# Down projection of a hybrid layer: finished blocks turned to frames by VectorE in 32x32 blocks that the stores put in place, instead of by TensorE

## Chip, cores and metric

One core of a Trainium2 chip. The time is the device time of one execution in microseconds (us). Engines: TensorE (PE, its weight loads PEld), VectorE (DVE), ScalarE (ACT), GpSimd (POOL), SyncE (SP). Times inside an execution come from the profile of one execution and count from the start of its span.

## The reference, cut to what matters

One streaming step of a layer for 512 prompt frames and 64 sample frames (576 together, 2048 channels, all float32): a projection into attention and convolution groups, an output projection, and a SwiGLU feed-forward. The change touches the last line alone:

```python
x = x + mix @ w_out
h2 = rmsnorm(x, g_norm2)
x = x + (jax.nn.silu(h2 @ w_gate) * (h2 @ w_up)) @ w_down     # w_down: 5632 x 2048
```

The result goes to two tensors, `y_prompt` (512 x 2048) and `y_sample` (64 x 2048), frame by row.

## The kernel before, in words

Everything is kept with channels on the 128 partitions and frames along the row, so the down phase ends with blocks of 128 channels x 288 frames that must be turned before they are stored as rows of frames.

**Work units.** The down phase computes 8 column groups `d` of 256 channels. Each gives four blocks `(c, i)`: `c` is which 128 of its channels, `i` which half of the frames (`HALVES`: 0 to 287 and 288 to 575). The hidden pairs arrive over time, so `DOWN` (L44) is a hand-written list of 37 visits `(d, first pair, last pair)`; a visit works on m pairs. The last eight visits, 29 to 36 here, finish the groups d = 0, 1, 3, 6, 7, 5, 2, 4 with m = 5, 5, 5, 5, 5, 6, 4, 4, and only they store. A group's multiplication is done by a seven-product (Strassen-Winograd) scheme: products 1 to 7, each of 3m matmuls (`multiply`, L400; three matmuls a pair, from a high and a low part of each operand). The order (L1517 to L1522) is, around visit n: (n+1, 1), (n, 3), (n, 4), (n+1, 2), (n+1, 6), (n+1, 7), (n+1, 5), and for the last visit (36, 4), (36, 3).

**What ends a block** (`run`, L421 to L477). Block (0,0) is done after product 2, (1,1) after product 5, (0,1) after product 3, (1,0) after product 4. DVE adds the PSUM result to the block (`add`, L449), POOL adds the copies `part` that ACT keeps (L451). Products 7 and 4 share one PSUM tile `psw`: 4 is accumulated upon 7, so TensorE may start product 4 only when DVE has read product 7 for block (1,1) (L449).

**Weights.** A visit's weights come in one transfer of m x 256 KB into one of two regions (`load_columns`, L327, on SP), as soon as the splits of products 3 and 4 of the visit that used the region are done. `prepare` (L357) makes the high part by ACT (L227) and the low part by DVE (L228) four products ahead (`AHEAD`, L1621), into four buffers; the weight sums of the scheme are DVE's too (L344 to L352).

**Order.** From the last gate and up unit on, the program order is each engine's order (`manual_schedule`, L1627): an instruction that waits holds up all that follows on its engine. DMAs issued from SP and ACT report on eight completion counters in turn; a DMA waits until the one eight before it has landed.

**The store** (`store_y`, L1579) is a generator in `Pipeline` (L73). One tick is one pair of a product (three matmuls); a generator runs when as many ticks have gone by as it yielded. Nine ticks after its block is done, TensorE turns it in three pieces against an identity matrix (L1598) into one of two PSUM tiles; three ticks on, ACT copies 256 frames back over the block (L1601) and the last 32 into one of four small tiles `obs` (L1603); four ticks on, the stores are issued: two on SP for i = 0 (L1606, L1589), four for i = 1, whose frames go over from `y_prompt` to `y_sample` at frame 512 (L1589, L1591). The stores of the last visit are shared among SP, ACT and POOL.

Of the kernel before, what the change touches and what calls it, by code (L numbers as in the profile page):

```python
# [10 lines left out]
F32 = mybir.dt.float32  # L11
# [5 lines left out]
P = 128  # L17
TP = 512
TS = 64
T = TP + TS  # L20
HALF = T // 2
HALVES = ((0, HALF), (HALF, T))
D = 2048
KD = D // P
NH = 8
# [10 lines left out]
NFP = NFF // 2  # L36
DC = D // 256
SLOTS = 7
# [63 lines left out]
def tile_hybrid_stream_step(  # L102
# [6 lines left out]
    nc = tc.nc  # L109
# [5 lines left out]
    yp, ys = y_prompt[0], y_sample[0]  # L115
# [24 lines left out]
    def misc(name):  # L140
        return ps_z.tile([P, 512], F32, tag="misc", name=name, bufs=2)
# [3 lines left out]
    for half in (1, 0):  # L145
        for c in range(D // 256):
            specs.append((w_out[half * AW : (half + 1) * AW, c * 256 : (c + 1) * 256]
# [7 lines left out]
    NU = len(gu)  # L155
# [38 lines left out]
    def next_weight():  # L194
        i = pos[0]
        pos[0] += 1
        end = first_block
        def pieces_of(j):
            hi, lo = weight_split(j)
            for a in range(0, 2048, 512):  # L200
                weight_parts(raws[j][:, :2048], hi, lo, a, a + 512, nc.vector)
                yield 7

        while len(raws) < min(i + 2, end):
            load_weight()
        if len(ready) <= i:
            split_weight(nc.vector)
        while len(raws) < min(i + 3, end):
            load_weight()
        if i + 1 < end:  # L210
            pipe.spawn(pieces_of(i + 1))
            pipe.run_due()
        out = ready[i]
        ready[i] = None
        return out
# [20 lines left out]
    ident = const.tile([P, P], F32, name="ident")  # L236
# [4 lines left out]
    rows = {}  # L241
# [72 lines left out]
    def load_columns(gone=(), one=False):  # L314

        free.extend(gone)
        while wanted and room(*wanted[0]) and (one or not hold):
            n, c = wanted.pop(0)
            one = False
            src, wide_, m = source(n, c)  # L320
            halves = room(n, c)
            for h in halves:
                free.remove(h)
            t = raw_tile[halves[0][0]]
            t = t[:, halves[0][1], :] if len(halves) == 1 else t.rearrange("p h e -> p (h e)")
            t = t[:, : 2 * m * wide_]
            nc.sync.dma_start(out=t.rearrange("p (k e) -> p k e", e=wide_), in_=src)  # L327
            if c is None:
                v = t.rearrange("p (j s h c) -> p j s h c", s=2, h=2, c=P)
                region[n, 0], region[n, 1] = (v[:, :, :, 0, :], halves), (v[:, :, :, 1, :], ())  # L330
            else:
                region[n, c] = t.rearrange("p (j s c) -> p j s c", s=2, c=P), halves
# [216 lines left out]
    def turn_x(kt, low=None):  # L549
# [25 lines left out]
        if q == 0:  # L575
            for (a, b), d in zip(HALVES, (b11[:, j], b12a[:, j] if j < NP - 1 else b12b)):
                nc.scalar.activation(out=d[:, 0, :], in_=st[:, 0, a:b], func=AF.Copy, scale=g)
# [54 lines left out]
    with tc.manual_schedule(engines={mybir.EngineType.Activation, mybir.EngineType.DVE, mybir.EngineType.SP}):  # L632
# [60 lines left out]
        for kt in range(KD + LAG):  # L693
# [22 lines left out]
            if kt in (7, 11, 17):  # L716
                j = (kt - 7) // 4
# [7 lines left out]
        for c in range(2):  # L725
            for i, (a, b) in enumerate(HALVES):
                if i:
# [12 lines left out]
        for kt in range(KD):  # L740
# [6 lines left out]
            if kt == 9:  # L747
                nc.vector.reduce_sum(out=ssr, in_=ssx, axis=mybir.AxisListType.X)
                nc.vector.tensor_scalar(out=ssr, in0=ssr, scalar1=1.0 / D, scalar2=EPS, op0=ALU.mult, op1=ALU.add)
                nc.gpsimd.tensor_tensor(out=rst, in0=ssr, in1=nhalf, op=ALU.pow)  # L750
# [15 lines left out]
    for c in range(2):  # L766
        for i, (a, b) in enumerate(HALVES):
            nc.scalar.copy(out=e1[c][:, a:b], in_=v1ps[c][i])
# [81 lines left out]
    def group_scale(acc_, bufs):  # L850
        for a, b in HALVES:
            ss = misc("ssg")[:, :HALF]
            mm(ss, oner.bitcast(F32), acc_[:, a:b], start=True, stop=True)
            yt = tmp.tile([P, 2, HALF], F32, tag="hl", name="ytg", bufs=bufs)
            y, t = yt[:, 0], yt[:, 1]
            nc.scalar.activation(out=ss, in_=ss, func=AF.Identity, scale=1.0 / (8 * P), bias=epsc)
            nc.scalar.activation(out=y, in_=ss, func=AF.Ln)
            nc.scalar.activation(out=y, in_=y, func=AF.Exp, scale=-0.5)
            nc.scalar.activation(out=t, in_=y, func=AF.Square)
            nc.vector.scalar_tensor_tensor(out=t, in0=t, scalar=-0.5, in1=ss, op0=ALU.mult, op1=ALU.mult)  # L860
            nc.vector.scalar_tensor_tensor(out=acc_[:, a:b], in0=t, scalar=1.5, in1=y, op0=ALU.add, op1=ALU.mult)
            yield 1
# [11 lines left out]
    def a_done(n, c, i, ps, part):  # L874
        kind, g = UNITS[n][:2]
        a, b = HALVES[i]
        if kind in ("v", "qk"):
# [189 lines left out]
    for h in range(NH):  # L1067
        t = tpool.tile([P, 2, T], F32R, tag=f"t{h}", name=f"mixa{h}")
# [5 lines left out]
    def out_proj(frame, R, after=None, before=None, first=None):  # L1074
        for c in range(D // 256):
            whi, wlo = first[0] if first and c == 0 else next_weight()
            load_x2()
            if before:
                before(c)
            for j in range(2):  # L1080
                kt = 2 * c + j
                for a, b in HALVES:
                    if first and kt == a == 0:
                        ps = first[1]
                    else:
                        ps = ps_pj.tile([P, HALF], F32, tag="pj", name="pjo")
                        product(ps, whi, wlo, slice(j * P, (j + 1) * P), frame, 8, a, b)
                    if first and c < PLAIN:
                        nc.vector.tensor_tensor(out=x2(kt)[:, a:b], in0=ps, in1=R[:, a:b], op=ALU.mult)
                        continue  # L1090


                    def finish_out(wait, ps=ps, kt=kt, a=a, b=b):
                        yield wait
                        nc.vector.tensor_tensor(out=ps, in0=ps, in1=R[:, a:b], op=ALU.mult)
                        nc.vector.tensor_tensor(out=x2(kt)[:, a:b], in0=ps, in1=x2(kt)[:, a:b], op=ALU.add)

                    pipe.spawn(finish_out(3 if after and kt == a == 0 else 0))
                    pipe.run_due()
                if first and j and c < PLAIN:  # L1100
                    nc.gpsimd.dma_start(out=x2t[c], in_=xt_dram[2 * c : 2 * c + 2].rearrange("k p t -> p k t"),
                                        accum_op=ALU.add)
                if after:
                    after(kt)
# [227 lines left out]
    down = {}  # L1332
# [52 lines left out]
    def before_b2(c):  # L1385
        if c == 3:
            load_columns([("B", 0), ("B", 1)])
        elif c == D // 256 - 2:
            load_columns([("A", 0)])
# [138 lines left out]
    for d, v in visits.items():  # L1528
        n = next(a for a, b in zip(v, v[1:]) if a >= NGU + 10 and b >= a + 4)
        residual.setdefault(n + 1, []).append(d)  # L1530
    acc = {}
# [47 lines left out]
    def store_y(n, c, i):  # L1579

        d = UNITS[n][1]
        src, cs, f0 = acc[d, c, i], slice((2 * d + c) * P, (2 * d + c + 1) * P), HALVES[i][0]
        r = HALF - 2 * P

        def put(f, ap, queue=nc.sync):

            rows, n_p = ap.shape[0], max(min(TP - f, ap.shape[0]), 0)
            if n_p:
                queue.dma_start(out=yp[f : f + n_p, cs], in_=ap[:n_p])  # L1589
            if n_p < rows:  # L1590
                queue.dma_start(out=ys[f + n_p - TP : f + rows - TP, cs], in_=ap[n_p:])  # L1591

        def work():
            yield 9
            po = misc("pot")[:, : 3 * P]
            for q in range(3):
                w = min(P, HALF - q * P)
                nc.tensor.transpose(po[:w, q * P : (q + 1) * P], src[:, q * P : q * P + w], ident)  # L1598
            yield 3
            ob = src[:, : 2 * P].rearrange("p (i c) -> p i c", c=P)  # L1600
            nc.scalar.copy(out=ob, in_=po[:, : 2 * P].rearrange("p (i c) -> p i c", c=P))  # L1601
            obs = down["pool"].tile([r, P], F32, tag="obs", name="obs", bufs=4)
            nc.scalar.copy(out=obs, in_=po[:r, 2 * P :])  # L1603
            yield 4
            if i == 0:
                nc.sync.dma_start(out=yp[: 2 * P, cs].rearrange("(i p) c -> p i c", p=P), in_=ob)  # L1606
            else:
                put(f0, ob[:, 0, :])
                put(f0 + P, ob[:, 1, :], nc.scalar if n == NU - 1 else nc.sync)
            put(f0 + 2 * P, obs, nc.gpsimd if n == NU - 1 else nc.sync)  # L1610

        pipe.spawn(work())


# [80 lines left out]
```

## Time and profile before

| | |
|---|---|
| time before, median of 3 runs | 2347.15 us (2346.91 to 2348.15) |
| the profiled execution | 2347.48 us, span 2345.8 us |
| TensorE clock granted | 1.0 throughout |
| first transposes of a finished block | 2228.6 us |
| end of the last product | 2339.39 us |
| last store issued | 2342.55 us |

The down phase adds to its first block at 1841 us; the blocks are turned and stored in its last 120 us. In the views of the profile, a tile's name stands for the tensor with numbers left out: `pot` is the PSUM tile of turned pieces, `acc`, `acc_z`, `acc_t`, `acc_ax` hold blocks, `whl` split weights, `raw_a` and `raw_b` the two weight regions, `psy`, `psw`, `psx` the PSUM tiles of products 1, 6, 5, 3, of 7 and 4, and of 2. SPq and ACTq are DMA issues of those engines, q1 and q10 their DMA queues, q0 is POOL's.

### The profile page before, as it was taken

How to read it: one execution, taken by the hardware profiler on the slowest of the kernel's cores; microseconds unless marked ns; L12 is line 12 of the kernel's file. 1: busy time of each engine (PE TensorE's matmuls, PEld its weight loads, DVE VectorE, ACT ScalarE, POOL GpSimd, SP SyncE). 2: the span in 40 equal slices, each digit the busy share in tenths (PEclk: the TensorE clock that was granted, in tenths of full speed). 3: DMA queues.
4: the chain of work that ended last, by engine and by line, in shares of the span. 5: the costliest groups of instructions: out<-in, count | busy, mean ns of one | idle time of the engine just before them, and what ended most of it. 6: DMA issues, size and time to landing. Idle time of an engine off the chain costs nothing. (4 is left out here: it accounts for less than half of the span.)

```text
span 2345.8 us, 43802 instructions
## 1 busy us (share of the span) xinstructions
PE 2332.0 (99%) x17561; PEld 2321.6 (99%) x17561; DVE 1940.0 (83%) x2834; ACT 1239.2 (53%) x2244; POOL 294.2 (13%) x374
## 2 busy tenths in 40 slices
PE   9999999999999999999999999999999999999999
PEld 8999999999999999999999999999999999999998
DVE  8889889797777898888888888888888778887875
ACT  8556656455887564444444444444444444444454
POOL 0211121120332320000000000000000002431211
PEclk9999999999999999999999999999999999999999
DMA  8444243436753454444444444444444937875642
GB/s 270 137 122 123 90 142 103 149 116 208 202 143 109 168 198 126 154 141 136 154 128 149 148 134 149 138 139 153 127 150 140 356 112 229 231 218 187 201 130 82
DMA packets 482867, 368.85 MB, mean 157 GB/s; under 512 B 11630, under 2 KB 465064, under 8 KB 482664
## 3 DMA queue, kind: packets, MB, share of 16 engines
q1 hardware_dynamic: 475848, 356.58, 47.5%
q0 software_dynamic: 6384, 9.21, 2.3%
q8 instruction: 137, 2.24, 0.4%
q14 instruction: 66, 0.54, 0.1%
q10 hardware_dynamic: 432, 0.27, 0.0%
HBM read 285.52 MB, written 80.49 MB: 156 GB/s over the span
## 5 line engine op out<-in xcount | busy, mean ns | idle before, releaser
L228 DVE TENSOR_TENSOR whl<-raw_a,whl 128x1024 fp32r<-128x1024 f32 (+4 forms) x384 | 435.8, 1135 | 61.2 <-ACT whl L227 59.9
L404 PE MATMUL psy<-t,whl 128*128 128x288 f32 x3000 | 449.8, 295 | 0.0
L227 ACT CAST whl<-raw_a 128x1024 fp32r<-128x1024 f32 (+4 forms) x384 | 360.0, 939 | 137.7 <-PE psx L404 46.4
L404 PE MATMUL psy<-h_s,whl 128*128 128x288 f32 x2766 | 417.4, 295 | 0.6 <-ACT part L427 0.6
L404 PEld LDWEIGHTS psy<-t,whl 128*128 128x128 f32 x3000 | 414.8, 188 | 0.2
L404 PE MATMUL psw<-t,whl 128*128 128x288 f32 x2688 | 390.3, 295 | 0.0
L404 PEld LDWEIGHTS psy<-h_s,whl 128*128 128x128 f32 x2766 | 383.7, 188 | 1.2 <-ACT part L427 1.1
L404 PEld LDWEIGHTS psw<-t,whl 128*128 128x128 f32 x2688 | 367.0, 188 | 0.2
L228 DVE TENSOR_TENSOR whl<-raw_b,whl 128x1024 fp32r<-128x1024 f32 (+5 forms) x234 | 253.3, 1083 | 88.0 <-ACT whl L227 87.1
L227 ACT CAST whl<-raw_b 128x1024 fp32r<-128x1024 f32 (+5 forms) x234 | 211.0, 904 | 211.0 <-issue 75.2
L427 ACT COPY part<-psy 128x288 f32<-128x288 f32 x309 | 122.8, 397 | 345.0 <-PE psy L404 343.8
L404 PE MATMUL psx<-h_s,whl 128*128 128x288 f32 x1164 | 170.9, 295 | 0.0
L227 ACT CAST whl<-s 128x1024 fp32r<-128x1024 f32 (+5 forms) x103 | 95.2, 925 | 122.8 <-PE psw L404 115.0
L404 PEld LDWEIGHTS psx<-h_s,whl 128*128 128x128 f32 x1164 | 159.8, 188 | 0.0
L404 PE MATMUL psy<-t12a,whl 128*128 128x288 f32 x1056 | 150.9, 296 | 0.0
L404 PE MATMUL psw<-t34a,whl 128*128 128x288 f32 x1056 | 150.6, 295 | 0.0
L404 PEld LDWEIGHTS psy<-t12a,whl 128*128 128x128 f32 x1056 | 143.5, 188 | 0.3
L404 PEld LDWEIGHTS psw<-t34a,whl 128*128 128x128 f32 x1056 | 143.7, 188 | 0.0
L228 DVE TENSOR_TENSOR whl<-s,whl 128x1024 fp32r<-128x1024 f32 (+5 forms) x103 | 109.8, 1066 | 20.2 <-ACT whl L227 19.5
L1439 POOL DMA_DIRECT2D hid_dram<-form x7 | 5.2, 738 | 954.1 <-DVE form L228 945.8
L223 PE MATMUL pjo<-mixc,whi 128*128 128x288 f32 x512 | 119.0, 300 | 0.0
L223 PE MATMUL pjo<-mixa,whi 128*128 128x288 f32 x512 | 102.8, 296 | 0.0
(591 smaller groups left out, 3953.3 us busy)
## 6 DMA issues: line engine op xcount, KB each, us to landing
hid_dram<-form SPq DMA_DIRECT2D x147, 288.0 KB, 2.8
raw_a<-in_w_in_dram SPq DMA_DIRECT2D x22, 1024.0 KB, 5.5
raw_b<-in_w_in_dram SPq DMA_DIRECT2D x22, 1024.0 KB, 6.1
raw_b<-in_w_gate_dram SPq DMA_DIRECT2D x22, 1024.0 KB, 7.8
raw_b<-in_w_up_dram SPq DMA_DIRECT2D x22, 1024.0 KB, 6.5
raw_a<-in_w_gate_dram SPq DMA_DIRECT2D x22, 1024.0 KB, 5.8
raw_a<-in_w_up_dram SPq DMA_DIRECT2D x22, 1024.0 KB, 5.5
h_s<-hid_dram SPq DMA_DIRECT2D x10, 2016.0 KB, 11.0
```

The source lines that it names most:

```text
L223: mm(ps, w_[:, k, csl], x_[:, a:b], start=(k == 0 and n == 0), stop=(k == nk - 1 and n == 2))
L227: cast = nc.scalar.copy(out=hi, in_=src)
L228: (lo_eng or nc.vector).tensor_tensor(out=lo, in0=src, in1=hi.bitcast(F32), op=ALU.subtract)
L404: mm(ps, whl[:, w_, j, :], x_, start=(start and j == 0 and q == 0), stop=(j == len(xs_) - 1 and q == 2), skip_group_check=True)
L427: nc.scalar.copy(out=t, in_=st["y"])
L1439: q.dma_start(out=hid_dram[fp][2 * n - 2 : 2 * n].rearrange("f p t -> p f t"), in_=t.bitcast(F32))
```

## The change

`store_y` no longer uses TensorE, PSUM or ACT's copies. Nine ticks after a block is done (five in the last visit), DVE's transpose instruction turns the 128 x 288 block in square pieces of 32 x 32 into one of two new tiles `ob` (128 x 288): within each piece rows and columns are exchanged, and the pieces stay where they are. The stores put the pieces in place: for each 32 partitions (32 channels) one store, whose runs are 32 channels, 128 bytes, long. A block with i = 0 has four stores of 288 runs, one with i = 1 four of 224 runs to `y_prompt` and four of 64 runs to `y_sample`. The stores are issued as soon as the transpose is written, without the seven ticks between. In the last visit every second chunk's stores go to ACT, and two small ones to POOL.

```diff
+BK = 32
         def work():
-            yield 9
-            po = misc("pot")[:, : 3 * P]
-            for q in range(3):
-                w = min(P, HALF - q * P)
-                nc.tensor.transpose(po[:w, q * P : (q + 1) * P], src[:, q * P : q * P + w], ident)
-            yield 3
-            ob = src[:, : 2 * P].rearrange("p (i c) -> p i c", c=P)
-            nc.scalar.copy(out=ob, in_=po[:, : 2 * P].rearrange("p (i c) -> p i c", c=P))
-            obs = down["pool"].tile([r, P], F32, tag="obs", name="obs", bufs=4)
-            nc.scalar.copy(out=obs, in_=po[:r, 2 * P :])
-            yield 4
-            if i == 0:
-                nc.sync.dma_start(out=yp[: 2 * P, cs].rearrange("(i p) c -> p i c", p=P), in_=ob)
-            else:
-                put(f0, ob[:, 0, :])
-                put(f0 + P, ob[:, 1, :], nc.scalar if n == NU - 1 else nc.sync)
-            put(f0 + 2 * P, obs, nc.gpsimd if n == NU - 1 else nc.sync)
+            yield 5 if ends else 9
+            ob = down["pool"].tile([P, HALF], F32, tag="ob", name="ob", bufs=2)
+            nc.vector.transpose(out=ob, in_=src)
+            for k in range(P // BK):
+                rows = ob[k * BK : (k + 1) * BK].rearrange("j (t c) -> j t c", c=BK)
+                cg = slice(c0 + k * BK, c0 + (k + 1) * BK)
+                queue = nc.scalar if ends and k % 2 else nc.sync
+                queue.dma_start(out=yp[f0 : f0 + n_p, cg].rearrange("(t j) c -> j t c", j=BK), in_=rows[:, : n_p // BK])
+                if n_p < HALF:
+                    queue = nc.gpsimd if ends and k < 2 else queue
+                    queue.dma_start(out=ys[:, cg].rearrange("(t j) c -> j t c", j=BK), in_=rows[:, n_p // BK :])
```

The instruction order of the built program shows what follows from it. TensorE's order is the old one without the 32 groups of three transposes. DVE's is the old one with 32 transposes, each of which waits for all stores of the block two before it (they read its `ob` tile). On SP the stores of a visit now come as 8 for block (0,1), 4 for (1,0), 4 for the next visit's (0,0), then the next weight load, then 8 for (1,1); before, the load stood ahead of the stores of (1,0) and (0,0).

More of the change, by code (lines that the diff above doesn't have):

```diff
@@ L1581, in store_y @@
         d = UNITS[n][1]
[L1582 to L1591, printed above, removed]
-        def work():
-            yield 9
-            po = misc("pot")[:, : 3 * P]
-            for q in range(3):
-                w = min(P, HALF - q * P)
-                nc.tensor.transpose(po[:w, q * P : (q + 1) * P], src[:, q * P : q * P + w], ident)
-            yield 3
-            ob = src[:, : 2 * P].rearrange("p (i c) -> p i c", c=P)
-            nc.scalar.copy(out=ob, in_=po[:, : 2 * P].rearrange("p (i c) -> p i c", c=P))
-            obs = down["pool"].tile([r, P], F32, tag="obs", name="obs", bufs=4)
-            nc.scalar.copy(out=obs, in_=po[:r, 2 * P :])
-            yield 4
-            if i == 0:
-                nc.sync.dma_start(out=yp[: 2 * P, cs].rearrange("(i p) c -> p i c", p=P), in_=ob)
-            else:
-                put(f0, ob[:, 0, :])
-                put(f0 + P, ob[:, 1, :], nc.scalar if n == NU - 1 else nc.sync)
-            put(f0 + 2 * P, obs, nc.gpsimd if n == NU - 1 else nc.sync)
+        src, c0, f0 = acc[d, c, i], (2 * d + c) * P, HALVES[i][0]
+        n_p = min(HALF, TP - f0)
+        ends = n == NU - 1
+        def work():
+            yield 5 if ends else 9
[9 more added lines that the diff above has]
+                    queue.dma_start(out=ys[:, cg].rearrange("(t j) c -> j t c", j=BK), in_=rows[:, n_p // BK :])
         pipe.spawn(work())
```

## Prediction

> **What bounds the kernel now.** I read the page's busy times first, then the chain that ended last in the final 146 us, then PE's own waits there, then busy times by stretch.
>
> ```profile
> span 2345.8 us, 43802 instructions
> PE 2332.0 (99%) x17561; PEld 2321.6 (99%) x17561; DVE 1940.0 (83%) x2834; ACT 1239.2 (53%) x2244; POOL 294.2 (13%) x374
> ```
> ```profile
> by line: PE psy L404 49.9%; PE psw L404 24.9%; PE psx L404 12.3%; PE pot L1598 6.7%; issue 1.0%; DVE raw_a L350 0.9%; DVE whl L228 0.9%; POOL out_dram L1591 0.4%; POOLq L1691 0.4%; POOL out_dram L1589 0.3%; ACT obs L1603 0.2%; ACT acc L1601
> ...
> 2250.77 2.01 PE psw L404 x15
> 2252.78 1.99 PE psx L404 x15
> 2254.77 0.33 PE pot L1598 x3
> ```
> ```profile
> engine line waited for: us in total, times, longest us
> PE pot L1598 <- ACT obs L1603: 0.3, 1, 0.3
> PE psx L404 <- DVE whl L228: 0.2, 1, 0.2
> ```
>
> TensorE is the bound to the end: from 2200 us on it waited 0.5 us in all, and the transposes stand on the chain, 0.33 us for three. A product of a five-pair visit is 2.0 us, so seven products and four groups make 15.3 us.
>
> ```profile
> core 0: us, PE busy (x) PEld busy (x) DVE busy (x) ACT busy (x) POOL busy (x), PEclk, DMA share, GB/s
> ...
> 2273.30:2288.60 15.30, 15.30 (x119) 15.25 (x118) 11.10 (x15) 7.79 (x19) 2.45 (x4) 1.00 0.46 142
> 2311.00:2323.50 12.50, 12.50 (x98) 12.45 (x97) 9.11 (x15) 5.57 (x14) 1.63 (x2) 1.00 0.09 25
> ```
>
> The first stretch is one five-pair visit, the second a four-pair one. DVE has 4.2 us spare in the one and 3.4 us in the other.
>
> **The change part by part.**
>
> *TensorE loses 32 groups.* The chain gives them 6.7% of 145.8 us, 9.8 us, or 30 times 0.33 = 9.9; the last two lie behind the last product. I take **-9.9 us**. A five-pair visit becomes 7 x 2.0 = 14.0 us, a four-pair one 7 x 1.6 = 11.2 us.
>
> *ACT loses 64 copies*, 0.37 and 0.25 us. ACT is 7.8 us busy in 15.3, so this is worth nothing by itself.
>
> ```profile
> L1603 ACT COPY obs<-pot x32: 248/250/257, 2229.8 to 2341.8; 32x128 f32<-32x128 f32 x32
> L1601 ACT COPY acc<-pot x20: 358/367/378, 2275.4 to 2341.6; 128x256 f32<-128x256 f32 x20
> ```
>
> *DVE gains 32 transposes.* The trace has none. The nearest row is an add of the same 128x288 block, 0.45 us; each further semaphore that an instruction waits for costs a row of 0.021 us, and a transpose waits for 4 to 8.
>
> ```profile
> L449 DVEq EVENT_SEMAPHORE  x53: 21/21/21, 1960.7 to 2337.8; - x53
> L449 DVE TENSOR_TENSOR acc<-psw,acc x36: 439/449/458, 1976.0 to 2337.9; 128x288 f32<-128x288 f32 x36
> ```
>
> Bounds: 0.35 us (one source instead of two, no waits) and 0.9 (half the rate). I take 0.45 + 0.1 = 0.55, nearest to the row. Four make 2.2 us: 11.1 + 2.2 = 13.3 of 14.0 us, and 9.1 + 2.2 = 11.3 of 11.2 (DVE's rows overlap by some hundredths each, so it just fits). What covers DVE is its lead: this split ends 4.7 us before TensorE takes it.
>
> ```profile
> 2260.28 0.82 DVE L228 TENSOR_TENSOR whl<-raw_a,whl 128x640 fp32r<-128x640 f32 x1
> ```
> ```profile
> 2265.83 1.07 PE L404 MATMUL psw<-t,whl 128*128 128x288 f32 x6
> ```
>
> [...]
>
> *SP gains stores.* A visit had 12; it now has 24 and up to one load.
>
> ```profile
> 2261.13 0.40 SPq L327 DMA_DIRECT2D raw_a<-in_w_down_dram  x1
> ...
> 2266.86 0.82 SPq L1589 DMA_DIRECT2D out_dram<-acc_ax  x2
> 2267.74 0.42 SPq L1591 DMA_DIRECT2D out_dram<-acc_ax  x1
> 2268.25 0.36 SPq L1591 DMA_DIRECT2D out_dram<-obs  x1
> ```
>
> Four issues take 1.75 us, 0.45 from one to the next where nothing waits (bounds 0.36 and 0.51). So 25 x 0.45 = 11.3 of 14.0 us, and 24 x 0.45 = 10.8 of 11.2: in the four-pair visits SP has almost no slack.
>
> *The DMA queues get 128-byte runs.* A block is 1152 runs of 128 B instead of 288 of 512 B, so a visit puts 4 x 1152 / 16 = 288 on each of the 16 engines. In the last 6 us only stores run:
>
> ```profile
> DMA packets 976, 0.44 MB, mean 74 GB/s; under 512 B 160, under 2 KB 976, under 8 KB 976
> ...
> q1 hardware_dynamic: 560, 0.26, 15.2%
> q10 hardware_dynamic: 320, 0.13, 8.5%
> ```
>
> The 160 small packets are 16 for each of ten DMAs, their completion signals: 48 of q1's, 64 of q10's. With 16 x 6 = 96 engine-us, 512a + 48b = 14.6 and 256a + 64b = 8.16, so a 512 B run costs a = 26.5 ns and a signal b = 21.5. Between them, a 128 B run is 22.7 ns; that is my value. Bounds: 6.6 (by bytes) and 53 (twice the 512 B run). Per visit and engine: 288 x 22.7 = 6.5 us, 24 signals 0.5, and a load 4.8 (0.46 x 15.3 = 7.0, less 72 x 26.5 and 13 x 21.5 ns), 11.8 of 14.0 us. It fits.
>
> [...] The trace shows no small run into memory, only that a signal is not dearer than 512 B. [...]
>
> *The new wait.* Each transpose waits until the stores of two blocks before have landed, and behind it DVE's splits and adds wait. Landing:
>
> ```profile
> DMA to landing us min/median/max: 1.6/1.7/6.2
> ```
>
> In a five-pair visit the tight one is (0,0), 4 us after (0,1), whose eight stores need 8 x 0.45 + 1.3 = 4.9 us: 0.9 us, inside the 4.7 us lead. For what comes through in visits 33 to 35 (a late load, carried lag) I take **+1.0**, bounds 0 and 3.
>
> At the end the lead does not help. Let E be the end of product (36,5); (36,4) follows, and waits until DVE has read product 7. In DVE's new order that add stands behind the transpose of (0,0) of visit 36, which waits for the stores of (0,1) of visit 35. Product (35,3) ended at E - 8.0 (five products of 1.6). Behind it come ACT's cast 0.6 and DVE's split 0.7 for (36,7), then the transpose of (1,1) of 35: stores can start at E - 6.1. Its 8 and the 8 of (0,1) take 16 x 0.45; the last is issued at E + 0.65 and lands at E + 2.3; transpose and add end at E + 3.3. TensorE stands 3.3 us if DVE is on time. In the four-pair visits SP has 0.4 us spare and DVE none, so a wait there is not made good: I add 1.7 us, one landing. **+5.0 us**, bounds 1.9 (issues of 0.36) and 7.
>
> *The tail.*
>
> ```profile
> 2337.80 1.59 PE psy L404 x12
> 2339.39 0.34 PE pot L1598 x3
> ```
> ```profile
> 2342.55 0.50 POOL L1591 DMA_DIRECT2D out_dram<-obs  x1
> ```
>
> From the end of the last product T = 2339.39 to the span's end are 6.4 us, the last store issued at T + 3.2. After: the transpose of (1,1) ends at T - 0.65 (behind the add for (36,4)); three issues per queue, landed at T + 2.0; only then the last transpose, to T + 2.5, and three issues, the last at T + 3.4 to T + 4.0. **+0.7**, bounds 0 and 1.5.
>
> *Sum* against the profiled 2347.48 us (span 2345.8 and 1.7 around it; 0.3 above the median): -9.9 + 1.0 + 5.0 + 0.7 = -3.2, **2344.3 us**.
>
> **The rivals.**
>
> *DVE is on time at the end* (faster): stall 3.3, tail 0.2, nothing in the visits: -9.9 + 3.5 = -6.4, 2341.1 us. For it: the 4.7 us lead and overlapping rows on DVE. Against: SP's 10.8 of 11.2.
>
> *DVE and SP become the bound in the short visits*: a transpose of 0.8 us and 0.50 us per issue make 24 x 0.50 = 12.0 us against 11.2; some 0.8 more in each of visits 34 to 36, the end stall 16 x 0.05 + 4 x 0.25 = 1.8 longer, and about 2 more lag: -3.2 + 2.4 + 1.8 + 2 = +3.0, about 2350.5.
>
> *The 128 B runs are dear* (slower). It decides where a visit's queue work passes 14.0 us: (14.0 - 4.8 - 0.5) / 288 = 30 ns. Then `ob` comes free late, DVE stands, and TensorE follows the queues. At 40 ns a visit with a load has 16.8 us, 2.8 too much, in about four, and 0.8 in three short ones: 2344.3 + 13.6, about 2358. At 53 ns all eight visits have 15.8 us, with five loads some 150 us from first to last store, where before were 110: about 2380. For it: the runs are a quarter of any in the trace. Against: a signal of a few bytes costs 21.5 ns.
>
> That nothing changes on TensorE is excluded: its order lacks exactly the 32 groups.
>
> **How the numbers follow.** Forecast 0.42, on-time rival 0.24, DVE-and-SP rival 0.12, dear runs 0.22. Range: low 2341.0, the on-time rival; high 2364, past the 40 ns case; left out are about 0.1 above and 0.07 below. 0.2% is 4.7 us (about what a measurement of this kernel can tell from no change): below 2342.5 faster, above 2351.8 slower. Faster: the on-time rival and a little of the forecast's case, 0.26. Slower: dear runs and half of DVE-and-SP, 0.29. Within: 0.45.
>
> **What would show it.** In the changed profile: no `pot` rows; five-pair visits of 14.0 us; a DVE transpose near 0.45 us; 24 issues a visit at 0.45; queue share near 11.8 / 14.0 = 0.84 in a visit with a load; PE waiting once, some 5 us, for the DVE add at the end. Wrong if PE waits in every visit for splits whose DVE waits end at DMAs (dear runs), or not at all at the end.

## The result, and the profile after

The changed kernel takes **2353.05 us** (median of 8 runs, 2352.13 to 2355.85), the kernel before 2346.76 us: a ratio of 1.003, 95% interval 1.0021 to 1.0039. It is slower by about 6 us, where the forecast was 2344.3 and a time within 0.2% of the kernel before was held likeliest. Line numbers from L23 on are higher by one up to `store_y`; its transpose is L1590, its stores to `y_prompt` L1595 and to `y_sample` L1598.

The profiled execution took 2352.73 us. First its page:

```profile
span 2351.0 us, 43717 instructions
PE 2325.3 (99%) x17465; PEld 2314.8 (98%) x17465; DVE 1951.7 (83%) x2866; ACT 1225.9 (52%) x2180; POOL 301.6 (13%) x374
```

TensorE has 96 instructions less and is busy 6.7 us less, but the span is 5.2 us longer. The chain of work that ended last, from 2200 us on, shows what came in; before, TensorE's lines held 94% of it.

```profile
by line: SPq L1598 12.4%; DMA out_dram<-ob 10.5%; SPq L1595 9.9%; DMA raw_b<-in_w_down_dram 8.8%; PE psy L405 7.6%; issue 7.6%; DVE whl L229 7.3%; DMA raw_a<-in_w_down_dram 5.6%; PE psw L405 5.3%; DVE raw_a L351 3.4%; ACT whl L228 2.9%; DVE
```

Now the issues of stores on SP, their landings and the landings of weight loads stand there. TensorE's own waits from 2200 us on (us in total, how many, the longest), 0.5 us before, are 11.3 us:

```profile
PE psw L405 <- DVE acc L450: 6.3, 1, 6.3
PE psy L405 <- ACT part L428: 3.5, 3, 2.6
PE psx L405 <- DVE whl L229: 0.8, 2, 0.6
PE psw L405 <- DVE acc_ax L450: 0.4, 1, 0.4
PE psw L405 <- DVE whl L229: 0.3, 1, 0.3
```

**The wait of 6.3 us** is the one at the end that the prediction described, before product (36,4). DVE's rows, then TensorE's:

```profile
2338.02 0.48 DVE L1590 STREAM_TRANSPOSE ob<-acc 128x288 f32<-128x288 f32 x1 [3.88 <-DMA out_dram<-ob]
2338.42 0.42 DVE L450 TENSOR_TENSOR acc<-psw,acc 128x288 f32<-128x288 f32 x1
```
```profile
2338.89 1.09 PE L405 MATMUL psw<-t,whl 128*128 128x288 f32 x3 [6.29 <-DVE acc L450]
...
2341.94 0.89 PE L405 MATMUL psy<-t,whl 128*128 128x288 f32 x3
```

The transpose stands 3.88 us for a buffer that stores still read, the add stands behind it, and TensorE waits for the add. TensorE's second row is the start of the next product, and shows something not foreseen: product (36,4) took 2341.94 - 2338.89 = 3.05 us instead of 1.6.

**The wait of 2.6 us** lies in a visit, where the prediction had 1.0 us in all. ACT's rows and TensorE's:

```profile
2287.34 0.83 ACT L228 CAST whl<-raw_b 128x768 fp32r<-128x768 f32 x1 [6.27 <-DMA raw_b<-in_w_down_dram]
2288.08 0.39 ACT L428 COPY part<-psy 128x288 f32<-128x288 f32 x1
```
```profile
2288.53 1.81 PE L405 MATMUL psy<-t,whl 128*128 128x288 f32 x6 [2.63 <-ACT part L428]
```

ACT stands 6.27 us for a weight load. The copy out of PSUM that TensorE needs is queued behind ACT's cast of those weights. The loads are late because SP issues them late. Its issues of loads, of eight stores ahead of one, and of the first store behind one:

```profile
2232.39 0.40 SPq L328 DMA_DIRECT2D raw_a<-in_w_down_dram  x1
...
2244.18 3.86 SPq L1595 DMA_DIRECT2D out_dram<-ob  x8
2248.14 0.40 SPq L328 DMA_DIRECT2D raw_b<-in_w_down_dram  x1
...
2264.31 0.40 SPq L328 DMA_DIRECT2D raw_a<-in_w_down_dram  x1
2267.24 0.32 SPq L1595 DMA_DIRECT2D out_dram<-ob  x1
...
2280.40 0.40 SPq L328 DMA_DIRECT2D raw_b<-in_w_down_dram  x1
```

Eight stores take 3.86 us, 0.48 each. The loads are 15.8, 16.2 and 16.1 us apart, where seven products take 14.0 us: each visit loses some 2 us of lead, and when the lead is used up TensorE waits. SP is not issuing all this time. Behind the load at 2264.31 it stands 2.5 us for the next transpose, which DVE reaches only at 2266.74, because it had stood for a buffer earlier and has worked without a gap since:

```profile
2261.51 0.48 DVE L1590 STREAM_TRANSPOSE ob<-acc_z 128x288 f32<-128x288 f32 x1 [2.07 <-DMA out_dram<-ob]
```

So in these visits the lap of 16 us runs through SP's issues and through the two buffers. Over all, DVE and ACT waited (DVE for buffers, ACT for loads):

```profile
DVE ob L1590 <- DMA out_dram<-ob: 17.1, 10, 3.9
ACT whl L228 <- DMA raw_b<-in_w_down_dram: 10.5, 2, 6.3
ACT whl L228 <- DMA raw_a<-in_w_down_dram: 8.3, 3, 4.0
```

**Where the 5.2 us of span come from.** The two profiles are not level when the stage begins: product 2 of visit 29, ahead of the first transpose, starts at 2222.25 before and at 2220.86 after, 1.4 us ahead. From there to the end of its last product (2339.39 and 2344.01) TensorE takes 117.1 us before and 123.2 after, 6.0 more. That is -9.9 for the matmuls, +11.1 for waits (11.3 less 0.2), +3.2 for matmuls at a lower clock, and 1.6 that is left. Of the 3.2, 1.8 is seen at the end: five groups of three matmuls, 2338.89 to 2342.66, took 3.77 us instead of 5 x 0.40 (12 matmuls in 1.59 us, in the chain of before). The other 1.4 lie behind the 2.63 us wait: four groups, 2288.53 to 2291.53, took 3.00 instead of 1.59. The granted clock (the third column from the end, before DMA share and GB/s) is low in both. Two rows of busy times by stretch:

```profile
2288.50:2290.50 2.00, 1.97 (x8) 1.97 (x9) 2.00 (x2) 1.23 (x2) 1.28 (x1) 0.50 0.24 38
2338.80:2340.60 1.80, 1.71 (x7) 1.71 (x8) 0.04 (x1) 0.40 (x1) 0.59 (x1) 0.50 0.65 109
```

The 1.6 lies beside the waits: the last group ahead of one and the first behind it take 0.1 to 0.2 us longer than others. From the last product's end to the span's end it is 7.0 us instead of 6.4. Sum: -9.9, in the visits + 4.8 of waits, + 1.4 of slow clock and + 1.6 beside the waits, at the end + 6.3 and + 1.8 of slow clock, + 0.6 in the tail: +6.6, less the 1.4 of head start = +5.2.

**The operations themselves are cheap.** The transpose (its mean is the last number of the first part, in ns), and the store queue from 2312 to 2336 us, in which next to nothing but stores ran:

```profile
L1590 DVE STREAM_TRANSPOSE ob<-acc 128x288 f32<-128x288 f32 x20 | 9.5, 473 | 13.0 <-DMA out_dram<-ob 13.0
```
```profile
q1 hardware_dynamic: 8144, 0.96, 24.8%
```

0.248 x 16 x 24 = 95.2 engine-us for 8144 packets. 42 DMAs were issued in the stretch; less 42 x 16 = 672 signals at 21.5 ns, 7472 runs of 128 B took 80.8 us, **10.8 ns a run**.

### The profile page after: what moved, and what is told of

It is laid out like the page before. It is cut to its first block, busy times and chain, and to the rows that moved or that the text cites. A ratio compares the mean times of both kernels' runs of the same rounds, so it can differ in the third digit from the quotient of the medians.

```text
span 2351.0 us, 43717 instructions
## 1 busy us (share of the span) xinstructions
PE 2325.3 (99%) x17465; PEld 2314.8 (98%) x17465; DVE 1951.7 (83%) x2866; ACT 1225.9 (52%) x2180; POOL 301.6 (13%) x374
## 5 line engine op out<-in xcount | busy, mean ns | idle before, releaser
L428 ACT COPY part<-psy 128x288 f32<-128x288 f32 x309 | 123.2, 399 | 350.8 <-PE psy L405 340.0
## 6 DMA issues: line engine op xcount, KB each, us to landing
h_s<-hid_dram SPq DMA_DIRECT2D x10, 2016.0 KB, 10.8
```

What stands on the lines that cost most here:

```text
L428: nc.scalar.copy(out=t, in_=st["y"])
```

## The experiments

Three theories stood at the start. **A**: the two `ob` buffers close a loop (stores, transpose, splits, next load). **B**: SP's queue is the bound, and the buffers only hand it on. **C**: VectorE's own work is the bound. Times are medians, ratios are to the kernel before on the same chip in the same session, with 95% intervals.

| run | what | us | ratio |
|---|---|---|---|
| in_place | no buffers | 2356.04 | 1.0041 (1.0027 to 1.0055) |
| load_act | loads on ACT | 2355.01 | 1.0038 (1.0025 to 1.0050) |
| both | both of these | 2353.04 | 1.0029 (1.0018 to 1.0041) |
| late00 | one transpose behind one add | 2351.83 | 1.0025 (1.0015 to 1.0034) |
| few | 10 issues a visit, 512 B, in wrong places | 2337.23 | 0.9958 (0.9946 to 0.9971) |
| long24 | 24 issues, 512 B, incomplete | 2351.35 | 1.0023 (1.0014 to 1.0032) |
| issues16 | 16 issues, 128 B, incomplete | 2339.51 | 0.9971 (0.9961 to 0.9982) |
| before24 | kernel before, 24 issues | 2349.81 | 1.0015 (1.0006 to 1.0024) |
| pool_half | half the stores on POOL | 2342.01 | 0.9981 (0.9973 to 0.9990) |
| ip_pool_half | that, in place | 2337.76 | 0.9967 (0.9954 to 0.9979) |
| ip_load_pool | in place, loads on POOL | 2371.83 | 1.0106 (1.0092 to 1.0120) |
| ip_end_pool | in place, last stores not on ACT | 2346.59 | 0.9998 (0.9990 to 1.0007) |
| end_pool | the same with buffers | 2356.52 | 1.0040 (1.0025 to 1.0056) |
| ip_end_pool_late | ip_end_pool, loads ahead | 2344.78 | 0.9993 (0.9984 to 1.0002) |
| stall30 | kernel before, VectorE held up | 2357.61 | one run |

### In place: the buffers taken away

```diff
-            ob = down["pool"].tile([P, HALF], F32, tag="ob", name="ob", bufs=2)
-            nc.vector.transpose(out=ob, in_=src)
+            ob = src
+            nc.vector.transpose(out=ob, in_=src)
```

> Each block is transposed in place, so that no transpose waits for an earlier block's stores; stores and loads keep their queues. The changed kernel: 2353.0 us, the one before: 2346.8. Theory A, the two ob buffers close the loop (stores, transpose, splits, next load): the 6.3 us wait of TensorE at the end, the 1.45 us that the slow product behind it takes longer, the 3.5 us of waits in the visits and 0.5 us of slow clock there go: about 2341, and DVE waits for no store. Theory B, SP's 24 issues of 0.485 us are the bound by themselves and the buffers only hand it on: the end wait goes, but the loads still stand behind 16 stores and come late, and the last stores leave SP no earlier than 2336 us: 2345 to 2346. Theory C, VectorE's own work is the bound: 2352 or more.

Measured 2356.0: not faster. By the medians it is 3 us slower than the changed kernel, but the intervals of the two ratios overlap. TensorE's row of waits, its last row, and SP's wait for stores:

```profile
PE psy L405 <- ACT part L428: 4.0, 3, 1.8
```
```profile
2334.77 0.55 PE L405 MATMUL psy<-h_s,whl 128*128 128x288 f32 x3
```
```profile
SPq L1595 <- DMA out_dram<-acc: 11.0, 4, 8.0
```

The wait at the end is gone. From product 2 of visit 29 (here 2223.34) to the end of the last product TensorE takes 112.0 us, 5.1 less than before the change and 11.2 less than after it: beside the 8.1 at the end, 3.1 of the visits' 7.8 went. But the span ends at 2354.8, 19.5 us behind the last product: the stores lag. **Theory A falls** as the one cause: without the buffers' loop the loads still come 15.0 to 16.0 us apart, and TensorE waits 4.0 us for copies that stand behind their casts. C falls too: VectorE's work is what it was, and TensorE is done earlier. B is left, but it gave 2345 to 2346; SP's 11.0 us of waits for stores stay unexplained here.

### The load on ACT, alone and in place

```diff
-            nc.sync.dma_start(out=t.rearrange("p (k e) -> p k e", e=wide_), in_=src)
+            (nc.scalar if n >= NU - 5 else nc.sync).dma_start(out=t.rearrange("p (k e) -> p k e", e=wide_), in_=src)
```

> Two ob buffers as in the changed kernel; the last five weight loads are issued by ACT instead of SP, so that they stand behind no store. If the load's place behind the stores on SP is what makes TensorE wait in the visits (A and B alike), the waits for psy and the slow clock behind them go, 4.0 us, and the wait at the end stays near 6.3: about 2349. If the visits wait because VectorE is held by its buffers and frees the raw halves late, or because the load itself takes long to land, 2352 to 2353.

> In place and loads on ACT together. Theory A: no more than in place alone gives, about 2341. Theory B: better than in place alone by the 3 to 4 us of waits for loads, about 2341 against 2345. Theory C: 2352 or more.

Measured 2355.0 and 2353.0, both misses. With the buffers (load_act) the loads on ACT still come 15.3 to 17.1 us apart: there they wait for VectorE's splits, the expectation's other case, and ACT idles up to 5.67 us ahead of one. ACT's rows in the second run:

```profile
2287.75 6.33 ACTq L328 DMA_DIRECT2D raw_a<-in_w_down_dram  x2
2294.18 0.40 ACT L428 COPY part<-psy 128x288 f32<-128x288 f32 x1 [10.51 <-DMA out_dram<-acc]
```

ACT waits for a store that SP issued, holds two loads for 6.33 us, and TensorE stands 7.4 us for the copy behind them. In the built program each DMA of SP and ACT signals on one of eight counters, given out in turn in the order of the program over both queues, and waits for the DMA that had its counter before. In the changed kernel the eighth store behind the load of 2280.40 stands 2.1 us for that load. So a load that has left SP's queue still waits for a store in it.

### The order at the end

```diff
-            yield 5 if ends else 9
+            yield 5 if ends and (c, i) != (0, 0) else 9
```

> Changed kernel with one instruction moved: in the last visit VectorE's add that (36,4) waits for stands ahead of the transpose of (0,0), not behind it. TensorE's wait of 6.3 us at the end goes, and the slow product with it (7.7 us of TensorE's time), in any case. If TensorE's end sets the end of the program (as the prediction had it): 2345.3. If the chain of stores through SP and the two buffers sets it by itself, most of this shows up again as a longer tail: the transpose of (0,0) still starts at 2338.0, three more blocks follow it at about 1.7 us each, and the end comes near 2347.5 of the span: about 2349.

Measured 2351.8; the 1.2 us below the changed kernel are within the intervals. (36,4) now waits 1.9 us, but the product after it waits 4.6 us. TensorE's row, and ACT's:

```profile
2340.17 0.92 PE L405 MATMUL psy<-t,whl 128*128 128x288 f32 x3 [4.61 <-ACT part L428]
```
```profile
2339.72 0.40 ACT L428 COPY part<-psy 128x288 f32<-128x288 f32 x1 [10.10 <-DVE acc L450]
```

That copy stands behind two stores which the change had given to ACT, and these wait for the moved transpose. The moved transpose still starts at 2338.2, where it was 2338.0: the stores of SP set the time, and the wait only moves.

### How many issues, or how long the runs

Few issues (the same bytes, in 512 B runs; frames and channels stand in wrong places of the output):

```diff
-            for k in range(P // BK):
...
+            if i == 0:
+                nc.sync.dma_start(out=yp[: 2 * P, cs].rearrange("(i p) c -> p i c", p=P), in_=o3)
+                nc.sync.dma_start(out=yp[2 * P : HALF, cs], in_=ob[:BK, BK + P :])
+            else:
+                (nc.scalar if ends else nc.sync).dma_start(out=yp[f0 : f0 + P, cs], in_=ob[:, :P])
+                nc.sync.dma_start(out=yp[f0 + P : TP, cs], in_=ob[: TP - f0 - P, P : 2 * P])
+                (nc.gpsimd if ends else nc.sync).dma_start(out=ys[:, cs], in_=ob[:TS, HALF - P :])
```

> The transposes on VectorE and the two ob buffers stay; a pair of blocks is stored by 2 and 3 DMAs with runs of 512 B instead of 4 and 8 with runs of 128 B. The same bytes leave, but the frames and columns stand in the wrong places of the output. The runs in place and with the loads elsewhere showed TensorE done 4 us earlier than before and the stores 19 us later: theory B, SP's queue is the bound, since 24 issues of 0.485 us, the load, and a wait of some 3 us in which the eighth DMA after a load waits for that load to land make 15 to 16 us a visit, against 14.0 of TensorE. With 10 issues a visit SP needs about 6 us: TensorE does not wait, and the time is that of before less the 9.9 us of matmuls, 2336 to 2338. If VectorE's transposes or the buffers cost by themselves: 2345 or more.

As many issues as in the change, with 512 B runs (78% of the bytes, in wrong places):

```diff
                 if i == 0:
+                    queue.dma_start(out=yp[2 * k * BK : 2 * (k + 1) * BK, cs].rearrange("(t j) c -> j t c", j=BK), in_=rows[:, : 2 * P].rearrange("j (t c) -> j t c", c=P))
                 else:
+                    queue.dma_start(out=yp[f0 + k * BK : f0 + (k + 1) * BK, cs], in_=rows[:, :P])
...
+                    queue.dma_start(out=ys[k * TS // 4 : (k + 1) * TS // 4, cs], in_=rows[: TS // 4, P : 2 * P])
```

> As the changed kernel in all but the stores' form: 4 and 8 issues per pair of blocks with runs of 512 B instead of 128 B. Of each block of frames 0 to 287 the last 32 frames are left out, of the others some more, and what is written stands in the wrong places. If the number of issues is the cause (B): as the changed kernel, 2350 to 2354. If the length of the runs is: as with few issues and 512 B, 2337.

Fewer issues with 128 B runs. The sample's frames are left out in 14 blocks of 32, not in 30 as the expectation has it, since only 16 blocks hold any:

```diff
-                if n_p < HALF:
+                if n_p < HALF and ends:
```

> Changed kernel without its stores of the sample's frames, but for the last visit's (64 of 576 frames are not written in 30 of 32 blocks): 16 issues a visit, 128 B runs, two buffers, load on SP. Theory B: SP needs 16 x 0.485 + 0.4 and up to 3.4 for the counter behind the load, 11.6 of 14.0 us, and at the end a transpose waits for 4 issues instead of 8: 2337 to 2340. If the buffers or the load's place behind stores hold VectorE whatever the count: 2350 or more.

Measured 2337.2, 2351.4 and 2339.5. TensorE's two largest waits with 24 issues of long runs:

```profile
PE psw L405 <- DVE acc L450: 6.4, 1, 6.4
PE psy L405 <- ACT part L428: 2.7, 3, 2.1
```

They are those of the changed kernel, 6.3 and 3.5; with 16 issues of short runs the largest is 1.1, with 10 of long ones 0.8. So the number of issues decides and not the length of the runs. With few issues, transposes and buffers and all, the program keeps nearly all of the 9.9 us: 9.5 by the medians.

The other way round, 24 issues in the kernel before:

```diff
-            if n_p:
-                queue.dma_start(out=yp[f : f + n_p, cs], in_=ap[:n_p])
+            for a in range(0, n_p, max((n_p + 1) // 2, 1)):
+                b = min(a + (n_p + 1) // 2, n_p)
+                queue.dma_start(out=yp[f + a : f + b, cs], in_=ap[a:b])
...
-                nc.sync.dma_start(out=yp[: 2 * P, cs].rearrange("(i p) c -> p i c", p=P), in_=ob)
+                for a, b in ((0, 48), (48, 96), (96, P)):
+                    nc.sync.dma_start(out=yp[: 2 * P, cs].rearrange("(i p) c -> p i c", p=P)[a:b], in_=ob[a:b])
```

> The kernel before, matmuls with the identity and all, with its stores cut into 24 issues a visit (4 and 8 per pair of blocks); runs of 512 B, right places. Theory B: SP then needs 15.4 to 15.9 us in a visit with a load, where TensorE needs 15.3, and has 0.8 us to spare in the short ones: a lag of a few us that shows in the tail, 2347 to 2351. If issues cost nothing: 2346.4.

Measured 2349.8, 0.15% above. TensorE waits no more than before. The loss is in the tail: from TensorE's last row to the span's end it is 8.0 us, before 4.9. (The spans differ by 0.4 us only, because this profile is 2.8 us ahead already at 2202 us.)

### Half the issues on POOL

```diff
-                queue = nc.scalar if ends and k % 2 else nc.sync
+                queue = (nc.scalar if ends else nc.gpsimd) if k % 2 else nc.sync
```

> Changed kernel, all its 128 B stores in place, but of the four column groups of a block two are issued by POOL instead of SP (in the last visit ACT, as it was). Theory B: SP has 12 issues a visit, 5.8 us, and no store of POOL counts on the loads' counters, so the loads go out in time and TensorE's waits go: 2337 to 2340, which is below before. If the number of runs or the two buffers is the bound: 2350 or more. If POOL's issues hold its own adds up: between.

Measured 2342.0, 0.19% below before: a little above the 2337 to 2340 that B gave, since one wait stays, 4.1 us for the add behind the transpose at the end:

```profile
PE psw L405 <- DVE acc L450: 4.1, 1, 4.1
```

With the transposes in place as well:

> Two of four column groups on POOL, and the transposes in place. The run with POOL alone had 2342.0 us, and TensorE waited once more than 0.3 us: 4.06 us at the end, behind a transpose that waited for a buffer. In place that wait goes, and the slow product behind it: 2342.0 - 4.1 - 1.5 = 2336.4 by theory B (with half the issues SP keeps up). If the stores still lag behind TensorE, the tail grows by what the wait gives back, as in place alone: 2341 or more.

Measured 2337.8, 0.33% below before. TensorE's waits from 2200 us on are as small as in the kernel before, 0.5 us in all:

```profile
PE psw L405 <- DVE acc L450: 0.3, 1, 0.3
PE psx L405 <- DVE whl L229: 0.2, 1, 0.2
```

This version leaves nothing out and beats both kernels. Its stores keep runs of 128 B.

### In place, loads on POOL

```diff
-            nc.sync.dma_start(out=t.rearrange("p (k e) -> p k e", e=wide_), in_=src)
+            for q_, a_, b_ in ((nc.gpsimd, 0, m), (nc.gpsimd, m, 2 * m)) if n >= NU - 5 else ((nc.sync, 0, 2 * m),): q_.dma_start(out=t.rearrange("p (k e) -> p k e", e=wide_)[:, a_:b_], in_=src[:, a_:b_])
```

> In place, and the last loads issued by POOL in two halves each; all stores stay on SP. It takes from SP the load and the wait of the eighth DMA behind it, and leaves the 24 issues: 11.7 us a visit against 14.0 and 11.2. If that wait is what lengthened the visits to 15 to 16 us, the stores keep up with TensorE but for some 1.5 us in the short visits: about 2340. If the 24 issues are too many by themselves: as in place with loads on ACT, about 2353.

Measured 2371.8, the worst of all, and it doesn't answer its question. POOL's rows:

```profile
2245.71 0.95 POOL L328 DMA_DIRECT2D raw_b<-in_w_down_dram  x1 [4.49 <-DMA out_dram<-acc_z]
2251.42 0.89 POOL L328 DMA_DIRECT2D raw_b<-in_w_down_dram  x1 [4.76 <-issue]
2252.33 0.81 POOL L452 TENSOR_TENSOR acc_t<-acc_t,part 128x288 f32<-128x288 f32 x1
```

The second half of a load starts 5.7 us after the first, and an add that POOL has to make stands behind both. A transpose waits for that add, and VectorE's splits for the transpose. A queue is free only if nothing that others need stands behind the issue.

### Why in place lagged: counters that the queues share

```diff
-                queue = nc.scalar if ends and k % 2 else nc.sync
+                queue = nc.gpsimd if ends and k % 2 else nc.sync
```

> In place alone took 2356.0 us, 10 us more than theory B gave (2345 to 2346), though TensorE was done at 2335.3: in its last 30 us SP waited 11.0 us, once 8.0, for stores of other queues. Here the last visit's stores that ACT issued are issued by POOL; all else is as in place. If SP's stores waited for ACT's because both count their landings on the same eight counters in turn, in the order of the program (theory B with counters), the 11 us go: 2345 to 2346. If SP's queue is simply too long: 2354 or more.

> The same edit in the changed kernel with its two buffers. There SP waits for no store of another queue at the end, but for the transposes, which wait for SP's own stores. If the counters play no part in the changed kernel's end: no change, 2352 to 2354. If they do: several us less.

In place: 2346.6 instead of 2356.0, as B with counters gave it; SP waits for no other store any more. In the changed kernel the same edit gives 2356.5, above the expected 2352 to 2354 and certainly not faster: its SP had waited 0.3 us for stores at the end, and POOL needs about 0.6 us for each of the 14 issues at the end, ACT 0.45. So the shared counters explain the run in place; in the changed kernel this edit shows nothing of them.

What stays in the run in place is TensorE's wait for late loads, and SP's waits for loads whose counters come round again:

```profile
PE psy L405 <- ACT part L428: 4.4, 3, 2.1
```
```profile
SPq L1598 <- DMA raw_b<-in_w_down_dram: 4.4, 2, 2.2
SPq L1598 <- DMA raw_a<-in_w_down_dram: 4.3, 2, 2.2
```

The change also moved the load: before, it stood ahead of eight stores, after it behind them. Put back, by seven ticks between transpose and stores:

```diff
-            ob = src
-            nc.vector.transpose(out=ob, in_=src)
+            ob = src
+            nc.vector.transpose(out=ob, in_=src); yield 0 if ends else 7
```

> As in place with the last visit's stores on POOL (2346.6 us), but the stores are issued seven ticks after the transpose, as the kernel before had it, so that on SP the weight load stands ahead of the 4 and 4 stores of blocks (1,0) and (0,0), not behind them. The number of issues stays. If the load's place behind these eight is what makes TensorE wait in the visits, its 4.4 us of waits for psy go. If the end follows TensorE: 2342. If it follows SP's queue, whose issues are as many as ever, the tail grows by most of it: 2344 to 2347.

Measured 2344.8; the 1.8 us below the run without it are within the spread. TensorE waits 0.7 us instead of 4.4 and is done at 2329.2, but the span ends 13.6 us later, at 2342.8. The last row of TensorE and SP from one load to the next:

```profile
2328.66 0.55 PE L405 MATMUL psy<-h_s,whl 128*128 128x288 f32 x3
```
```profile
2260.28 0.40 SPq L328 DMA_DIRECT2D raw_a<-in_w_down_dram  x1
2260.72 2.74 SPq L1595 DMA_DIRECT2D out_dram<-acc_t  x4
2263.51 3.26 SPq L1595 DMA_DIRECT2D out_dram<-acc_z  x4
...
2274.01 1.67 SPq L1598 DMA_DIRECT2D out_dram<-acc_z  x1
2275.78 0.40 SPq L328 DMA_DIRECT2D raw_b<-in_w_down_dram  x1
```

SP issues without a gap for 15.5 us, where TensorE needs 14.0: eight stores right behind a load took 6.0 us instead of 3.9, and one later 1.67 instead of 0.44. So, without the buffers, the load's place is what makes TensorE wait, the number of issues is what makes the end late, and taking away one of them leaves the other.

### The clock behind a wait

```diff
             if later:
+                if n == NU - 1:
+                    idle = down["pool"].tile([P, P], F32, tag="idle", name="idle", bufs=1)
+                    nc.vector.memset(idle, 0.0)
+                    for _ in range(30):
+                        nc.vector.tensor_tensor(out=idle, in0=idle, in1=idle, op=ALU.add)
                 add(1, 1, st["w"])
```

> The kernel before, with 30 small additions on VectorE (128 x 128, results unused) put ahead of the add that the last but one product waits for. TensorE is made to idle some 6 us there and nothing else changes. If TensorE's clock falls after an idle of this length, the product behind it takes 3.0 us instead of 1.6 with a granted clock near 0.5, and the program is longer by the wait and about 1.5 us; if the slow product in the changed kernel had another cause (the stores' traffic), it takes 1.6.

TensorE's rows, and a stretch of busy times:

```profile
2344.21 1.09 PE L404 MATMUL psw<-t,whl 128*128 128x288 f32 x3 [8.39 <-DVE acc L449]
...
2347.25 0.92 PE L404 MATMUL psy<-t,whl 128*128 128x288 f32 x3
```
```profile
2344.20:2346.00 1.80, 1.79 (x7) 1.79 (x8) 0.00 (x0) 0.00 (x0) 1.30 (x2) 0.50 0.00 0
```

The wait was 8.4 us, not 6; the product took 3.04 us at a granted clock of 0.50, with no DMA traffic at all in that stretch. So a wait was enough here for a slow product, and the slow product of the changed kernel needs no other cause. This is one execution, read from its trace alone.

## Why the prediction was wrong, step by step

- **TensorE loses 32 groups, -9.9**: right. With few issues nearly all of it shows, 9.5 us.
- **VectorE gains 32 transposes of 0.55 us**: nearly right, 0.47. With few issues the same transposes cost nothing that shows.
- **128 B runs at 22.7 ns**: too dear, they take 10.8. No run shows the third rival's 40 and 53 ns, and it falls; long24 shows it by itself. A run of 128 B did cost more per byte than one of 512 B here (0.084 against 0.052 ns), but less per run (10.8 against 26.5 ns).
- **"So 25 x 0.45 = 11.3 of 14.0 us"**: this is the step that failed, and with it the term for the visits that rested on SP's slack. The pitch was about right (0.48), but it was taken from four issues that had the queue to themselves, and multiplied. With a load in the queue SP needs 15.5 us even where it issues without a gap (ip_end_pool_late): issues right behind a load took longer (there 6.0 us for eight instead of 3.9), and when the counters came round, a store waited for the load to land (2.1 us behind the load of 2280.40 in the changed kernel). In the changed kernel a load comes 16 us after the one before: 12 us are issues at 0.48, 1.5 one long issue, and 2.5 SP's wait for a transpose that the buffers made late. One row of SP's waits in the kernel before hinted at stores that wait for a load:

```profile
SPq L1591 <- DMA raw_a<-in_w_down_dram: 0.8, 1, 0.8
```

- **The visits, +1.0 (bounds 0 and 3)**: measured 7.8, of which 4.8 are waits, 1.4 slow clock behind one of them and 1.6 beside them. This is most of what the sum lacks. The order of SP was known: the load had gone behind eight stores. The prediction counted the issues and did not follow what the load's lateness does to the next split; ip_end_pool_late shows that its place alone takes 3.7 of 4.4 us of waits away.
- **The stall at the end, +5.0 (bounds 1.9 and 7)**: the mechanism was right, the wait itself is 6.3. The slow clock behind it, 1.8, was not foreseen at all.
- **The tail, +0.7**: right, 0.6.
- **The rivals**: the second, "DVE and SP become the bound in the short visits" (2350.5), is nearest by its time. Its SP half is what happens, but already in the five-pair visits, through the loads; its DVE half is not: the 0.8 us a transpose were the author's assumption, no run shows them, and 0.47 was measured. That 2353 lies inside the stated range is luck: the range reached that high for the dear runs, which fall.
- **Several things hold at once**, and the number of issues on SP weighs most. Repairs that leave 24 issues on SP gave little: without buffers, 2344.8 at best. Fewer issues on SP with the buffers kept gave 2337.2 and 2339.5 (with incomplete or misplaced stores) and, with half of them on POOL, 2342.0; half on POOL and in place, 2337.8.

What is left open: how much of SP's 15 to 16 us is the longer issue behind a load and how much the counters was read from rows, not separated by a run; ip_load_pool was meant for it and failed by POOL's adds. Why issues behind a load took longer was not tried.

## What to carry to other kernels

Work moved off the busiest engine came back here as DMA issues, 24 a visit on SP instead of 12. Add up the issuing queue in the stretch as the engines are added up, with the loads that share it and with the waits for counters, and ask what the first thing is that now stands behind more than it did; a queue with 0.45 us an issue and 20% to spare on paper had none with the load in it. Where several waits replace one another, an experiment that takes one away can come out no faster, as in place did; take two away at once before a theory is given up.

## What the runs showed of the hardware

- TensorE's granted clock fell to 0.50 in some of its waits, and what came behind them ran slowly. Between 2200 us and the end of the last product the changed kernel has two such stretches, 3.4 us from 2288.1 on (the wait of 2.63 us) and 6.8 us from 2335.8 on (the wait of 6.29 us); in the kernel before, which waited 0.5 us in all, there is none. In stall30, behind 8.39 us, the clock was 0.50 from 2344.2 to 2346.0. The length of the wait alone did not decide: behind one of 2.09 us (ip_end_pool) the matmuls were slow, behind one of 2.70 us (end_pool) they were not. The rows of ip_end_pool and end_pool, with six matmuls each:

```profile
2289.07 1.41 PE L405 MATMUL psy<-t,whl 128*128 128x288 f32 x6 [2.09 <-ACT part L428]
```
```profile
2290.19 1.06 PE L405 MATMUL psy<-t,whl 128*128 128x288 f32 x6 [2.70 <-ACT part L428]
```

  The groups of three behind them took 0.92 and 0.56 us. What decides was not shown. On top of the wait such a stretch cost 1.4 us (the 2.63 us wait) and 1.8 us (the end of the changed kernel).
- A store in 128 B runs took the queues 10.8 ns a run (the changed kernel, 2312 to 2336 us), less than half of the 26.5 ns of a 512 B run in the kernel before; the bytes per ns were still lower, 11.9 against 19.3.
- VectorE turned 128 x 288 fp32 elements in squares of 32 in 0.47 us, about as long as an add of the same block (0.45).
